# Splitting float32 weights inside the DMA transfers instead of on ScalarE and VectorE, in a two-layer transformer trunk

## The chip, the cores and the metric

One Trainium2 chip; the kernel runs on one of its cores. The metric is the device time in microseconds (us) of one execution. A core has TensorE (PE, matrix products; PEld is its weight loads), VectorE (DVE), ScalarE (ACT), GpSimd (POOL), SyncE (SP) and 16 DMA engines that all queues share. SP and ACT hand transfers to queue q1 and q10, POOL hands them to queue q0.

## What is computed

Two layers over 256 latent and 256 context tokens of width 1024. Each layer is a half step of a SwiGLU feed-forward net, a token mixing with four attention branches, and another half step. Each of the three starts with an RMS norm, scaled and shifted per feature. The last layer needs its second half step, and the queries of its mixing, for the latent half alone.

```python
D_MODEL, SEQ, CTX_LEN, DEPTH, D_FF = 1024, 256, 256, 2, 2816

def rmsnorm(x, g, eps=EPS):
    x32 = x.astype(jnp.float32)
    y = x32 * lax.rsqrt(jnp.mean(x32 * x32, axis=-1, keepdims=True) + eps)
    return (y * g.astype(jnp.float32)).astype(x.dtype)

def modulate(h, g, shift, scale):
    return rmsnorm(h, g) * (1 + scale) + shift

def swiglu(u, w_gu, w_down):
    g, up = jnp.split(u @ w_gu, 2, axis=-1)
    return (jax.nn.silu(g) * up) @ w_down

def gated_merge(u, ys, w_branch, w_gate, b_gate, w_out):
    terms = []
    for i, y in enumerate(ys):
        y = y.reshape(y.shape[:2] + (BRANCH_W,))
        terms.append(jax.nn.sigmoid(u @ w_gate[i] + b_gate[i]) * (y @ w_branch[i]))
    ...
    return merged @ w_out
```

All of it is float32. The kernel multiplies in the shorter format fp32r, and so writes each float32 operand as a high part (the value rounded to fp32r) and a low part (the rest). A product is the sum of three: high by high, high by low, low by high.

## The kernel before

Features lie on the 128 partitions and tokens along the free dimension: 512 columns where both halves run, 256 where the latent half runs alone. A **block** is 512 KB of weight, [128, 1024] (some are 384 KB and smaller). A full block makes 24 products, eight slices of 128 features by three (`mm3`, L132 to L138), and is used once. There are 414 blocks, all through `weights` (L119): SP loads a block into `wraw` (three buffers), ACT rounds it into `whi` (L127), DVE subtracts to get `wlo` (L128), and PE uses both. `whi` and `wlo` have five buffers each, so that weights are made up to five blocks ahead of PE.

The stages, by the time at which they run in the profiled execution: an opening (to about 47 us), the first half step of layer 0 (to about 390), its mixing (to 890), its second half step (to 1257), the first half step of layer 1 (to 1630), its mixing with 256 query columns (to about 1955), and its second half step with 256 columns. During the half steps of 512 columns but for the mixing, SP also loads 512 KB blocks `wa` of the modulation weights, which DVE multiplies and sums itself (L298).

Each engine works off its own list in order; a scheduler fixes the lists when the kernel is built, from the order in which the code asks for the work and from when buffers come free. A row `[waits PE_49]` in such a list says that the instruction waits for a count of PE's; DMASW and DMAHW are counts of transfers.

The factors 1/sqrt of the norms (`rsqrt_cols`, L140) are three Newton steps on tiles of 2 to 8 columns; by default POOL does them in twelve small instructions, in places VectorE in nine (`eng=nc.vector`). POOL also adds the branches (`merged`, L529), makes low parts of some heads (`ds`, L620), adds bias masks (`nab`, L708), and issues the SBUF-to-SBUF copies `kh`, `kl`, `mkh`, `mkl`.

## Time and profile before

| | |
|---|---|
| median of 2 runs | 2156.12 us (2155.53 to 2156.71) |
| span of the profiled execution, first to last instruction | 2153.2 us |
| PE busy | 2107.4 us, 98% |
| DVE busy | 1469.2 us, 68% |
| ACT busy | 911.8 us, 42% |
| POOL busy | 180.7 us, 8% |
| moved by DMA | 301.52 MB, 140 GB/s in the mean |

The profiled execution has no time of its own beside its span: the median of the runs is 2.9 us above the span, which is what lies around it. PE is close to always busy; the other engines and the DMA are busy in part, and by stage very differently, so their shares have to be read stage by stage.

### The profile page before, as it was taken

Reading aid. Unit: us, or ns where it says so; the run is one execution under the profiler, and the core shown is the slowest. Engines: PE = TensorE matmul, PEld = TensorE weight load, DVE = VectorE, ACT = ScalarE, POOL = GpSimd, SP = SyncE. Lnnn points to the kernel's source line nnn. Section 1 sums busy time; section 2 is a strip of 40 time slices with the busy share of each in tenths; the row PEclk is TensorE's granted clock in tenths of the full one; section 3 lists DMA queues with packets and bytes.
Section 4 is the critical chain, followed back from the end, with each engine's and each line's share of the span. In section 5 each row is a group of like instructions: output and inputs, shape, how many; then the busy total and the mean of one; then the engine's idle time right before and its main releaser. Section 6 shows DMA issues by size and latency. Waiting matters only on the chain.

```text
span 2153.2 us, 31572 instructions
## 1 busy us (share of the span) xinstructions
PE 2107.4 (98%) x12130; PEld 1805.8 (84%) x12130; DVE 1469.2 (68%) x2639; ACT 911.8 (42%) x1456; POOL 180.7 (8%) x322
## 2 busy tenths in 40 slices
PE   7999999999999999999999999999999999999998
PEld 5888888987777877988888898888889888999998
DVE  6776767678767665566665558767667887787655
ACT  3422222467655563432222233222225776765443
POOL 0000000110012112100000010000002433120000
PEclk9999999999999999999999999999999999999999
DMA  8555554241232223245444336555542335355553
GB/s 331 173 178 178 177 176 150 69 121 47 66 100 73 88 66 118 92 157 156 140 154 150 105 118 203 179 176 186 165 127 90 105 106 138 128 168 171 192 183 102
DMA packets 95207, 301.52 MB, mean 140 GB/s; under 512 B 18640, under 2 KB 20048, under 8 KB 94672
## 3 DMA queue, kind: packets, MB, share of 16 engines
q1 hardware_dynamic: 92080, 295.10, 43.0%
q0 software_dynamic: 2688, 4.20, 1.0%
q8 instruction: 96, 1.57, 0.3%
q14 instruction: 55, 0.45, 0.1%
q10 hardware_dynamic: 288, 0.20, 0.0%
HBM read 294.21 MB, written 1.05 MB: 137 GB/s over the span
## 4 chain that ended last, share of the span: by engine, by line
PE 89%; DVE 5%; ACT 2%; issue 1%; POOL 1%; DMA 1%; SPq 0%; DVEq 0%; POOLq 0%; ACTq 0%
PE pgu L134 13%; PE pgu L137 13%; PE pgu L138 13%; PE pd L137 6%; PE pd L138 6%; PE pd L134 6%; PE pgt L134 4%; PE pgt L137 4%; PE pgt L138 4%; PE av L789 2%; PE pj L134 2%; PE pj L137 2%; PE pj L138 2%; PE psS L735 2%; PE tps L775 1%
## 5 line engine op out<-in xcount | busy, mean ns | idle before, releaser
L127 ACT CAST whi<-wraw 128x1024 fp32r<-128x1024 f32 (+2 forms) x414 | 423.1, 1024 | 993.8 <-PE pgu L137 434.7
L128 DVE TENSOR_TENSOR wlo<-wraw,whi 128x1024 fp32r<-128x1024 f32 (+2 forms) x414 | 495.2, 1197 | 160.6 <-ACT whi L127 141.5
L134 PE MATMUL pgu<-uh,whi 128*128 128x512 f32 (+1 forms) x1440 | 511.9, 357 | 1.4 <-ACT sg L357 0.9
L137 PE MATMUL pgu<-ul,whi 128*128 128x512 f32 (+1 forms) x1440 | 512.7, 356 | 0.6 <-DVE ul L230 0.4
L138 PE MATMUL pgu<-uh,wlo 128*128 128x512 f32 (+1 forms) x1440 | 512.2, 356 | 0.0
L298 DVE SCALAR_TENSOR_TENSOR junk<-wa,sbc 128x1024 f32<-128x1024 f32 x256 | 312.3, 1220 | 3.1
L134 PEld LDWEIGHTS pgu<-uh,whi 128*128 128x128 f32 x1440 | 271.1, 189 | 43.4 <-issue 2.5
L137 PEld LDWEIGHTS pgu<-ul,whi 128*128 128x128 f32 x1440 | 272.1, 189 | 39.4 <-DVE ul L230 1.1
L138 PEld LDWEIGHTS pgu<-uh,wlo 128*128 128x128 f32 x1440 | 272.1, 189 | 39.1 <-DVE wlo L128 0.3
L137 PE MATMUL pd<-al,whi 128*128 128x512 f32 (+1 forms) x794 | 273.4, 344 | 0.2 <-DVE al L372 0.2
L134 PE MATMUL pd<-ah,whi 128*128 128x512 f32 (+1 forms) x794 | 273.5, 345 | 0.0
L138 PE MATMUL pd<-ah,wlo 128*128 128x512 f32 (+1 forms) x794 | 273.1, 344 | 0.0
L134 PE MATMUL pgt<-uh,whi 128*128 128x512 f32 (+1 forms) x512 | 176.5, 345 | 0.4 <-ACT cacc L548 0.4
L358 DVE TENSOR_TENSOR af<-sg,pgu 128x512 f32<-128x512 f32 (+1 forms) x86 | 53.6, 625 | 179.5 <-PE pgu L138 179.5
L137 PE MATMUL pgt<-ul,whi 128*128 128x512 f32 (+1 forms) x512 | 174.1, 340 | 0.0
L138 PE MATMUL pgt<-uh,wlo 128*128 128x512 f32 (+1 forms) x512 | 173.8, 339 | 0.0
L137 PEld LDWEIGHTS pd<-al,whi 128*128 128x128 f32 x794 | 149.3, 188 | 20.9 <-DVE al L372 0.9
L134 PEld LDWEIGHTS pd<-ah,whi 128*128 128x128 f32 x794 | 149.2, 188 | 20.0
L138 PEld LDWEIGHTS pd<-ah,wlo 128*128 128x128 f32 x794 | 149.1, 188 | 19.9
L336 DVE SCALAR_TENSOR_TENSOR h<-pd,mod,h 128x256 f32<-128x256 f32 x168 | 76.4, 480 | 105.7 <-PE pd L138 105.3
L148 POOL TENSOR_TENSOR rq<-ry 128x2 f32<-128x2 f32 (+2 forms) x48 | 12.1, 252 | 1252.5 <-DVE ry L146 1241.6
L134 PEld LDWEIGHTS pgt<-uh,whi 128*128 128x128 f32 x512 | 97.6, 191 | 13.2 <-issue 3.3
(240 smaller groups left out, 3125.2 us busy)
## 6 DMA issues: line engine op xcount, KB each, us to landing
wraw<-wgu SPq DMA_DIRECT2D x176, 512.0 KB, 3.3
wa<-wada SPq DMA_DIRECT2D x128, 512.0 KB, 4.2
wraw<-wd SPq DMA_DIRECT2D x64, 512.0 KB, 3.6
wraw<-wgate SPq DMA_DIRECT2D x64, 512.0 KB, 3.3
wraw<-win SPq DMA_DIRECT2D x28, 512.0 KB, 3.3
wraw<-wd SPq DMA_DIRECT2D x32, 384.0 KB, 3.1
w<-wada SPq DMA_DIRECT2D x16, 512.0 KB, 8.0
wraw<-wbr SPq DMA_DIRECT2D x16, 512.0 KB, 3.3
```

What stands on the lines that cost most here:

```text
L127: nc.scalar.copy(hi[:, :n], raw[:, :n])
L128: nc.vector.tensor_sub(lo[:, :n], raw[:, :n], hi[:, :n])
L134: ins = nc.tensor.matmul(ps, lh, rh, start=start, stop=False)
L137: nc.tensor.matmul(ps, lh, rl, start=False, stop=False)
L138: nc.tensor.matmul(ps, ll, rh, start=False, stop=stop)
L148: eng.tensor_mul(q[:, :n], y[:, :n], y[:, :n])
L298: ins = nc.vector.scalar_tensor_tensor(junk, w, 1.0, sbc[:, v], op0=ALU.mult, op1=ALU.mult, accum_out=m[:, t, v:v + 1])
L336: nc.vector.scalar_tensor_tensor(h[k][:, hv[0]:hv[1]], ps[:, off:off + S], gate[:, k, v:v + 1], h[k][:, hv[0]:hv[1]], op0=ALU.mult, op1=AL ...
L358: nc.vector.tensor_mul(af[:, :ntok], sg[:, :ntok], pu[:, :ntok])
L735: nc.tensor.matmul(ps[:, :nk], q_[:, q0:q0 + P], k_[:, self.k0:T], start=z == 0, stop=z == len(qs) - 1 and not bias_mm)
L775: nc.tensor.transpose(tps[:, b], self.p[:, b * P:(b + 1) * P], ident)
L789: nc.tensor.matmul(av[un.qt * 64:(un.qt + 1) * 64], V[br](u0.k0 // P + b, hd), un.pT[:, b], start=b == 0, stop=b == kt - 1)
```

## The change

`weights` no longer loads a block once. POOL issues a transfer from HBM into `whi`, which rounds on its way; ACT writes the negative of `whi` into `wlo`; POOL issues a second transfer of the same block, which adds the weight onto `wlo`. The buffer `wraw` is gone, and `whi` and `wlo` have six buffers instead of five. The Newton steps run on VectorE everywhere. The rest of the diff takes out comments. Line numbers after it are two or three lower: L125 and L127 are the transfers, L126 the negation, L132, L135 and L136 the products.

```diff
-    wp = es.enter_context(tc.tile_pool(name="wp", bufs=5))
+    wp = es.enter_context(tc.tile_pool(name="wp", bufs=6))
...
     def weights(src, shape):
         n = shape[1] * shape[2]
-        raw = wp.tile([P, 1024], F32, name="wraw", tag="wraw", bufs=3)
-        rv = raw[:, :n].rearrange("p (k c) -> p k c", k=shape[1])
-        nc.sync.dma_start(rv, src)
         hi = wp.tile([P, 1024], F32R, name="whi", tag="whi")
         lo = wp.tile([P, 1024], F32R, name="wlo", tag="wlo")
-        nc.scalar.copy(hi[:, :n], raw[:, :n])
-        nc.vector.tensor_sub(lo[:, :n], raw[:, :n], hi[:, :n])
-        return (hi[:, :n].rearrange("p (k c) -> p k c", k=shape[1]),
-                lo[:, :n].rearrange("p (k c) -> p k c", k=shape[1]))
+        hv, lv = [x[:, :n].rearrange("p (k c) -> p k c", k=shape[1]) for x in (hi, lo)]
+        nc.gpsimd.dma_start(hv, src)
+        nc.scalar.activation(lo[:, :n], hi[:, :n], AF.Copy, scale=-1.0)
+        nc.gpsimd.dma_start(lv, src, accum_op=ALU.add)
+        return hv, lv
...
-    def rms_cols(parts, ntok, dim, eps, heads=1, eng=nc.gpsimd, pin=False):
+    def rms_cols(parts, ntok, dim, eps, heads=1, eng=nc.vector, pin=False):
...
-        def cols(self, stats, hv, eng=nc.gpsimd):
+        def cols(self, stats, hv, eng=nc.vector):
...
-        def rest(self, stats, hv, between, eng=nc.gpsimd, rs=None):
+        def rest(self, stats, hv, between, eng=nc.vector, rs=None):
```

What this does to the lists is shown at three places. First the opening. SP's list before, where `wraw` are the blocks of weight and `w0` those of the first modulation:

```order
L1000 DMA w0_183<-wada0 128x1024 [waits DMAHW1_49]
L1000 DMA w0_189<-wada0 128x1024 [waits DMAHW2_49]
L124 DMA wraw_195<-wgu1 128x1024 [waits DMAHW3_49]
L124 DMA wraw_201<-wgu1 128x1024 [waits DMAHW4_49]
L1000 DMA w0_237<-wada0 128x1024 [waits DMAHW5_49]
L1000 DMA w0_243<-wada0 128x1024 [waits DMAHW6_49]
L1000 DMA w0_272<-wada0 128x1024 [waits DMAHW7_49]
L1000 DMA w0_278<-wada0 128x1024 [waits DMAHW0_49]
```

The two blocks of weight stand behind the first two `w0`, in one queue with all of them. POOL's list at the same place after the change (`ident` is a constant that POOL makes):

```order
L125 DMA whi_195<-wgu1 128x1024
masks.py:199 ISA
masks.py:199 AFFINE_SELECT ident_79<-ident_79 128x128 [waits Pool_49]
L127 DMA wlo_196<-wgu1 128x1024 [waits Activation_49]
L125 DMA whi_200<-wgu1 128x1024
L125 DMA whi_388<-wgu1 128x1024
L125 DMA whi_393<-wgu1 128x1024
L127 DMA wlo_201<-wgu1 128x1024 [waits Activation_49]
L127 DMA wlo_389<-wgu1 128x1024 [waits Activation_49]
L127 DMA wlo_394<-wgu1 128x1024 [waits Activation_49]
```

Eight transfers of four blocks now stand at the head of a queue of their own, beside SP's.

Next a stretch of the first half step of layer 0, SP's list before (`wgu1` are weights of the first half step, `wada` those of the modulation):

```order
L124 DMA wraw_1711<-wgu1 128x1024 [waits DMAHW2_49,DVE_49]
L124 DMA wraw_1718<-wgu1 128x1024 [waits DMAHW4_49,DVE_49]
L295 DMA wa_1547<-wada 128x1024 [waits DMAHW5_49,DVE_49]
L124 DMA wraw_1795<-wgu1 128x1024 [waits DMAHW6_49,DVE_49]
L124 DMA wraw_1802<-wgu1 128x1024 [waits DMAHW0_49,DVE_49]
L295 DMA wa_1623<-wada 128x1024 [waits DMAHW7_49,DVE_49]
L124 DMA wraw_1877<-wgu1 128x1024 [waits DMAHW1_49,DVE_49]
L295 DMA wa_1629<-wada 128x1024 [waits DMAHW2_49,DVE_49]
L124 DMA wraw_1884<-wgu1 128x1024 [waits DMAHW3_49,DVE_49]
```

A block is one row here, held back until a buffer `wraw` comes free. POOL's list in that half step after the change:

```order
L125 DMA whi_1451<-wgu1 128x1024 [waits DMASW6_49,PE_49]
L127 DMA wlo_1452<-wgu1 128x1024 [waits DMASW7_49,Activation_49]
L125 DMA whi_1525<-wgu1 128x1024 [waits DMASW0_49,PE_49]
L125 DMA whi_1531<-wgu1 128x1024 [waits DMASW1_49,PE_49]
L127 DMA wlo_1526<-wgu1 128x1024 [waits DMASW2_49,Activation_49]
L127 DMA wlo_1532<-wgu1 128x1024 [waits DMASW3_49,Activation_49]
L125 DMA whi_1605<-wgu1 128x1024 [waits DMASW4_49,PE_49]
L127 DMA wlo_1606<-wgu1 128x1024 [waits DMASW5_49,PE_49,Activation_49]
L125 DMA whi_1611<-wgu1 128x1024 [waits DMASW6_49,PE_49]
```

A block is two rows now, and the second (`wlo`) waits for ACT's negation, with the next `whi` queued behind it: first one block by itself (`whi`, `wlo`), then two together (`whi`, `whi`, `wlo`, `wlo`), and so on in threes.

Last the second half step of layer 1, with 256 columns. SP's list before:

```order
L124 DMA wraw_19228<-wgu2 128x1024 [waits DMAHW6_49,DVE_49]
L124 DMA wraw_19235<-wgu2 128x1024 [waits DMAHW7_49,DVE_49]
L124 DMA wraw_19298<-wgu2 128x1024 [waits DMAHW0_49,DVE_49]
L124 DMA wraw_19305<-wgu2 128x1024 [waits DMAHW1_49,DVE_49]
L124 DMA wraw_19368<-wgu2 128x1024 [waits DMAHW2_49,DVE_49]
L124 DMA wraw_19375<-wgu2 128x1024 [waits DMAHW3_49,DVE_49]
L124 DMA wraw_19438<-wgu2 128x1024 [waits DMAHW4_49,DVE_49]
```

Here too a block is one row and waits for nothing but a free buffer. POOL's list there after the change:

```order
L125 DMA whi_19328<-wgu2 128x1024 [waits DMASW6_49,PE_49]
L125 DMA whi_19390<-wgu2 128x1024 [waits DMASW7_49,PE_49]
L125 DMA whi_19396<-wgu2 128x1024 [waits DMASW0_49,PE_49]
L127 DMA wlo_19329<-wgu2 128x1024 [waits DMASW1_49,Activation_49]
L127 DMA wlo_19391<-wgu2 128x1024 [waits DMASW2_49,Activation_49]
L127 DMA wlo_19397<-wgu2 128x1024 [waits DMASW3_49,Activation_49]
L125 DMA whi_19458<-wgu2 128x1024 [waits DMASW4_49,PE_49]
L125 DMA whi_19464<-wgu2 128x1024 [waits DMASW5_49,PE_49]
L125 DMA whi_19526<-wgu2 128x1024 [waits DMASW6_49,PE_49]
```

Here three `whi` go out together and then three `wlo`, so that the next three `whi` stand behind the last of three negations.

## Rows read from the trace of the kernel before

**Rows 1.** The page, busy us and instructions of each engine.

```profile
PE 2107.4 (98%) x12130; PEld 1805.8 (84%) x12130; DVE 1469.2 (68%) x2639; ACT 911.8 (42%) x1456; POOL 180.7 (8%) x322
```

**Rows 2.** The page, the chain that ended last, by engine.

```profile
PE 89%; DVE 5%; ACT 2%; issue 1%; POOL 1%; DMA 1%; SPq 0%; DVEq 0%; POOLq 0%; ACTq 0%
```

**Rows 3.** The page, costliest groups: the split of the weights.

```profile
L127 ACT CAST whi<-wraw 128x1024 fp32r<-128x1024 f32 (+2 forms) x414 | 423.1, 1024 | 993.8 <-PE pgu L137 434.7
L128 DVE TENSOR_TENSOR wlo<-wraw,whi 128x1024 fp32r<-128x1024 f32 (+2 forms) x414 | 495.2, 1197 | 160.6 <-ACT whi L127 141.5
```

**Rows 4.** Busy us of the engines, clock, DMA share and rate in seven stretches.

```profile
core 0: us, PE busy (x) PEld busy (x) DVE busy (x) ACT busy (x) POOL busy (x), PEclk, DMA share, GB/s
0.00:53.80 53.80, 39.18 (x259) 27.13 (x260) 32.71 (x95) 20.95 (x33) 0.70 (x6) 1.00 0.88 331
60.00:380.00 320.00, 320.00 (x1414) 263.11 (x1413) 229.20 (x351) 88.22 (x113) 0.00 (x0) 1.00 0.55 173
400.00:880.00 480.00, 472.04 (x2628) 383.38 (x2627) 326.21 (x683) 269.77 (x491) 71.12 (x112) 1.00 0.28 85
900.00:1250.00 350.00, 349.56 (x1646) 291.87 (x1645) 209.65 (x320) 97.85 (x131) 2.41 (x12) 1.00 0.44 140
1290.00:1620.00 330.00, 329.56 (x1480) 271.95 (x1479) 233.54 (x354) 90.93 (x115) 0.00 (x0) 1.00 0.54 171
1660.00:1950.00 290.00, 282.94 (x2137) 257.84 (x2137) 233.18 (x474) 198.74 (x349) 83.08 (x120) 0.99 0.44 133
2000.00:2100.00 100.00, 100.00 (x838) 99.79 (x837) 57.42 (x69) 42.26 (x54) 0.00 (x0) 1.00 0.58 185
```

**Rows 5.** PE's own waits: us in total, times, longest.

```profile
PE ps L177 <- POOL ry L155: 5.2, 4, 1.9
PE tps L775 <- DVE pexp L764: 7.8, 11, 1.9
```

**Rows 6.** Line L127 in six stretches: count, duration ns, first and last start.

```profile
L127 ACT CAST whi<-wraw x5: 1032/1045/1052, 14.6 to 42.2; 128x1024 fp32r<-128x1024 f32 x5
L127 ACT CAST whi<-wraw x60: 835/1053/1057, 61.2 to 376.8; 128x1024 fp32r<-128x1024 f32 x52, 128x768 fp32r<-128x768 f32 x8
L127 ACT CAST whi<-wraw x67: 622/1049/1111, 400.7 to 869.2; 128x1024 fp32r<-128x1024 f32 x58, 128x768 fp32r<-128x768 f32 x5, 128x864 fp32r<-128x864 f32 x2, 128x576 fp32r<-128x576 f32 x1
L127 ACT CAST whi<-wraw x64: 835/1053/1061, 899.3 to 1244.3; 128x1024 fp32r<-128x1024 f32 x56, 128x768 fp32r<-128x768 f32 x8
L127 ACT CAST whi<-wraw x63: 835/1053/1061, 1292.9 to 1614.4; 128x1024 fp32r<-128x1024 f32 x55, 128x768 fp32r<-128x768 f32 x8
L127 ACT CAST whi<-wraw x67: 622/1047/1064, 1664.1 to 1948.5; 128x1024 fp32r<-128x1024 f32 x61, 128x768 fp32r<-128x768 f32 x5, 128x512 fp32r<-128x512 f32 x1
```

**Rows 7.** DMA issues (count, size, us to landing): all; 60 to 380; 900 to 1250.

```profile
wraw<-wgu SPq DMA_DIRECT2D x176, 512.0 KB, 3.3
wa<-wada SPq DMA_DIRECT2D x46, 512.0 KB, 4.2
wa<-wada SPq DMA_DIRECT2D x30, 512.0 KB, 3.4
```

**Rows 8.** DMA queues in 1660 to 1950: packets, MB, share of 16 engines.

```profile
q1 hardware_dynamic: 14206, 36.04, 40.2%
q0 software_dynamic: 1344, 2.10, 3.5%
```

**Rows 9.** POOL's issue of a DMA (busy, mean ns, then idle before it).

```profile
L665 POOL DMA_DIRECT2D kh<-kh x12 | 6.7, 561 | 78.7 <-ACT kh L662 78.7
```

**Rows 10.** Timeline 388 to 398: the same POOL instruction beside DVE and alone.

```profile
390.72 1.23 DVE L128 TENSOR_TENSOR wlo<-wraw,whi 128x1024 fp32r<-128x1024 f32 x1 [0.21 <-ACT whi L127]
390.87 1.13 POOL L153 TENSOR_TENSOR rq<-rq,rv 128x2 f32<-128x2 f32 x1
392.96 0.20 POOL L153 TENSOR_TENSOR rq<-rq,rv 128x2 f32<-128x2 f32 x1
```

## Prediction

> **What bounds the kernel now.** I read first the page's busy times: PE works 2107.4 of 2153.2 us, DVE 1469.2, POOL 180.7 [rows 1]. Then the chain that ended last: 89% of it is PE, 5% DVE, 1% POOL [rows 2]. So PE's pace sets the time, and all that a faster VectorE could give back lies in 46 us of PE's idle time, 2.1%. The table by stretches says where it lies [rows 4]: 14.6 us in the first 53.8, 8 in the mixing of layer 0, 7 in that of layer 1, next to none in the half steps. The same table says what carries the change: the DMA engines are 0.88 busy in the opening, about 0.55 in the first half steps, 0.28 and 0.44 in the mixings, 0.58 in the last half step. The last reading is of the counts of blocks in each stretch [rows 6], from which PE's pace per block follows.
>
> A full block is 24 products. In 60 to 380 a product takes 320 us / 1414 = 0.226 us, so a block 5.43; in the last half step 100 / 838 = 0.119, so a block 2.86 [rows 4]. In the mixings the stretch divided by its blocks is 480 / 67 = 7.16 us (layer 0) and 290 / 67 = 4.33 us (layer 1) [rows 4, 6]. A weight path that needs longer than this for each block stops PE.
>
> **What the change takes away.** DVE loses 414 subtractions, 495.2 us [rows 3]. PE hardly waited for them, so they are worth little in time. The negation takes the place of ACT's rounding; I cost it at that row's 1.05 us. The rstd chains leave POOL, where PE waited 5.2 us for them in all; its waits for DVE's `pexp` come to 7.8 us [rows 5]. I take 10 us of gain for both, between 0 and 21 (POOL's 1% of the chain, [rows 2]).
>
> **What it adds: the price of a transfer.** The DMA engines' full rate is 331 GB/s / 0.88 = 376 GB/s in the busiest stretch [rows 4], so a block (524,288 bytes) takes 1.39 us of all 16. From issue to landing a load takes 3.3 us [rows 7], hence 1.91 us beyond the moving. An issue on POOL takes 0.56 us [rows 9]. The first transfer I cost like a load, 1.39. The second adds onto what lies in `wlo`, and no row shows such a transfer. It costs at least what it costs to load the weight, 1.39 us. The upper bound is the load plus a whole copy from SBUF to SBUF: queue q0 moved 2.10 MB of such copies in 3.5% of 290 us, 10.2 us of all engines, so 2.53 us a block [rows 8], 3.92 together. The old `wlo` has to be read besides the weight, but written only once, so I take two loads, 2.78 us.
>
> The Trainium skill has the rule for this: in "Collectives: The Full Stack", section "The bandwidth ceiling: the fold count and why AG ≠ RS ≠ AR", an add in the DMA path is slower because it reads two sources on one ring, and not because of the adding; it gives 62.28 GB/s for a copy against 32.35 with an add, a factor of 1.93. By that factor the second transfer would take 2.68 us and my sum would come out some 25 us lower. No run shown here has such a transfer.
>
> **The round trip on POOL's list.** DMA capacity alone is not the limit in the early half steps, but POOL's list is in order, and a `wlo` waits there for ACT with the next `whi` behind it. I follow one group of three blocks as the list has it (whi, wlo, whi, whi, wlo, wlo), the DMA taken as one server of 376 GB/s. First `whi`: moved 0.56 to 1.95, landed 3.86, negated 4.91, its `wlo` issued 5.47 and moved until 8.25. The second and third `whi` stand behind that and are moved until 9.64 and 11.03; the second lands 11.55, is negated 12.60, its `wlo` goes out 13.16 and moves until 15.94, the third until 18.72, where the next group begins. A group thus takes 18.16 us, 6.05 a block, against PE's 5.43: 0.62 too long. The modulation loads lie on top. There are 46 for 60 blocks [rows 6, 7], so 1.07 us a block, of which half should fall into the DMA's gaps (1.95 to 5.47 and 11.03 to 13.16 above, 5.65 us a group): 0.53 more. In 60 to 380 that is 1.15 x 60 = 69 us; in 900 to 1250, with 30 such loads, 0.95 x 64 = 61; in 1290 to 1620, with again 46, 1.13 x 63 = 71. Together 201. Each of these stages begins with weights five blocks ahead, 27 us, of which a block's way through both transfers uses 10; the other 17 are eaten up before PE waits. 201 - 51 = **150 us**.
>
> **Last half step.** The group is three `whi`, then three `wlo`. The first `wlo` goes out at 5.47, the three are moved until 13.81, where the next group begins: 13.25 us, 4.42 a block against 2.86. This is now plainly the DMA's own limit (4.17 of moving a block). The code asks for 68 blocks here; four are wanted early and some three more lie ready, and eight of the rest are 384 KB, which leaves 59 full ones: 1.56 x 59 = 92, less 4 of lead, **88 us**.
>
> **Mixing of layer 1.** A block needs 4.17 us of DMA where PE's pace is 4.33, so it just fits. But POOL's own adds, 83 us in this stretch [rows 4], now stand in one list with the transfers. If they were all in the way it would cost 83 us, if none 0; **30 us**, since they leave gaps of POOL's 290. In layer 0's mixing 6.05 is under 7.16: nothing.
>
> **Opening.** The DMA has 12% of 53.8 us free there, 6.5. Five blocks were rounded in it [rows 6]; with six begun, six second transfers and one more first one are 18.1 us. PE waits for the `w0` behind them: **12 us**, between 0 (hidden in the 14.6 us of idle PE) and 18.
>
> **Sum.** 150 + 88 + 30 + 12 - 10 = 270 us on 2153.2, so a span of 2423; with 2.9 us around it **2426 us**, 12.5% more. What a measurement can tell here from no change is about 2%, 2113 to 2199 us.
>
> With the second transfer at 1.39 us the group of the half steps takes 4.66 a block (5.19 with half the modulation loads), which fits; the last half step 3.03 against 2.86, 5 us after the lead; the mixing 15, the opening 3: 2153 + 13 + 3 = **2169**. At 3.92 the group takes 7.19 a block, 366 us in the three half steps; the last one 5.56, 156; the mixing 0.98 x 67 + 30 = 96; the opening 18: **2782**.
>
> **Rivals.** (1) *The adding transfer moves at the price of a plain load.* Then every round trip fits PE's pace and the time is 2169, not slower than before. It decides at the second transfer's moving time: with it under about 1.6 us PE stays the bound. For it: nothing here shows that reading SBUF and HBM for one transfer cannot overlap. Against it: a 512 KB load already runs the engines at their full rate.
> (2) *Rounding on the way costs as much as adding.* The first transfer would take 2.78 us and the second 4.17, 6.95 a block and 2877 us for 414 blocks, above PE's pace in all stages but one; with the modulation loads about **3000 us**. Nothing in the trace speaks for or against, since none of its transfers changes the format.
> (3) *POOL's issues are held up by VectorE.* The same POOL instruction takes 1.13 us beside a subtraction of DVE's and 0.20 alone [rows 10]. Were each issue 0.9 us longer, 1.48, the group would take 5.36 us a block even with plain loads; with half the modulation loads 0.46 too long, 35 us after the lead, and the time about **2210**. Against it: `kh` issues take 0.56 us in the mean with DVE busy around them [rows 9]. In the Trainium skill, "SBUF — State Buffer", section "Who interferes with whom", transfers issued from GpSimd starve for descriptors while VectorE, in a two-port mode (a float32 copy within SBUF, for one), holds the ports that both share; by that rule the cost falls where VectorE copies, and no run shown here has a POOL issue that starved.
> (4) *The idle of PE goes.* All of it would be 46 us, 2110: faster by just over 2%. The weights would have to come sooner than now with twice the transfers.
>
> **How the numbers follow.** My forecast (second transfer at 2 to 3.9 us, 2250 to 2800) 0.48; rival 1 0.24; rival 2 0.18; rival 3 0.07; rival 4 0.03. The time is that of the likeliest, 2426. The range goes down to 2165, past most of rival 1, and up to 2850, just above the upper bound of the add; what is left out is rival 2, the lower part of rival 1 and rival 4. Slower by over 2%: 0.48 + 0.18 + 0.07 and a quarter of rival 1, 0.79; within 2%: 0.18; faster: 0.03.
>
> **What the profile after should show.** DMA share near 0.9 or more in the half steps, and 1.0 with PE idle in 2000 onward; PE waiting for DMA `wlo`, which it never did for weights; queue q0 with some 420 MB in place of 4.20; L127 landing some 1.5 us later than L125; L126 at about 1.05 us; DVE near 980 us. PE should stay whole in layer 0's mixing. If q0's `wlo` land as fast as `whi`, rival 1 holds; if `whi` themselves take 5 us or more from an idle DMA, rival 2; if POOL's issues exceed 1 us, rival 3. I am wrong altogether if PE's idle lies at POOL's own instructions rather than at transfers: then the list is at fault and not the DMA.

## The result, and where the time went

The kernel after takes **2662.16 us** (2660.36 to 2663.97, 2 runs) against 2156.12 (2155.53 to 2156.71): a ratio of **1.2344**, 95% interval 1.2308 to 1.238. It is slower, as forecast and inside the range; the forecast of 2426 us had about half of the 506 us that were lost. The profiled execution has a span of 2658.6 us.

The page of the kernel after, in the order of [rows 1]: busy time and share of PE, the granted clock and the DMA share in 40 slices, then the queues.

```profile
PE 2259.5 (85%) x12130; PEld 1901.9 (72%) x12130; DVE 1040.8 (39%) x2369; ACT 909.9 (34%) x1458; POOL 693.1 (26%) x958
...
PEclk8989898999999999989999898989889989898887
DMA  9887877574566667677787778888767789999997
...
q0 software_dynamic: 121920, 424.73, 68.1%
```

PE has 399.1 us of idle time (2658.6 - 2259.5) in place of 45.8, so 353 of the 505 us of span are new idle time. The other 152 are a surprise: PE's *busy* time has grown from 2107.4 to 2259.5 us with the same 12130 products. The clock line says why: it now falls to 8 again and again, where the page before has 9 in every slice.

```profile
PEclk9999999999999999999999999999999999999999
```

The mean granted clock is 0.997 before and 0.923 after. PE's busy time multiplied by it is 2101 us before and 2086 after, so the lower clock accounts for the growth.

The table by stages (the columns as in [rows 4]) has its borders at the products of the norms' sums (`acc`, L162, L164 before). Before, these stand at 389.6, 886.5, 1259.2, 1627.2 and 1950.6 us.

```profile
core 0: us, PE busy (x) PEld busy (x) DVE busy (x) ACT busy (x) POOL busy (x), PEclk, DMA share, GB/s
0.00:494.30 494.30, 402.02 (x1778) 317.46 (x1778) 197.85 (x396) 117.91 (x159) 99.62 (x145) 0.91 0.81 219
494.30:1044.60 550.30, 506.76 (x2754) 410.36 (x2754) 272.99 (x686) 275.48 (x502) 149.51 (x194) 0.96 0.62 141
1044.60:1503.50 458.90, 393.51 (x1833) 323.80 (x1833) 149.49 (x295) 104.99 (x144) 97.37 (x137) 0.93 0.75 190
1503.50:1957.10 453.60, 387.58 (x1772) 317.63 (x1772) 188.73 (x361) 106.63 (x145) 96.26 (x135) 0.92 0.79 206
1957.10:2350.10 393.00, 338.97 (x2390) 309.32 (x2391) 183.40 (x506) 213.93 (x378) 156.75 (x216) 0.92 0.83 193
2350.10:2658.60 308.50, 230.68 (x1606) 223.31 (x1604) 48.31 (x130) 90.93 (x130) 93.61 (x132) 0.86 0.92 223
```

Length less PE busy is the idle time of a stage; the same view of the trace before gives the other side. In us:

| stage | longer by | of it PE idle | of it PE busy | forecast |
|---|---|---|---|---|
| opening and first half step | 104.7 | 77.7 | 27.0 | 12 + 52 |
| mixing, layer 0 | 53.4 | 34.2 | 19.2 | 0 |
| second half step | 86.2 | 64.9 | 21.3 | 44 |
| first half step, layer 1 | 85.6 | 63.2 | 22.4 | 54 |
| mixing, layer 1 | 69.6 | 46.0 | 23.6 | 30 |
| last half step | 105.9 | 67.2 | 38.7 | 88 |

(The 52, 44 and 54 are the prediction's 69, 61 and 71 less 17 each, its 150.)

The waits of PE (us, times, longest), which in [rows 5] had no weight in them:

```profile
PE pd L132 <- ACT ah L369: 123.1, 19, 15.8
PE pgu L136 <- DMA wlo<-wgu: 60.0, 33, 3.9
PE pgu L132 <- ACT sg L355: 32.7, 12, 5.4
PE av L787 <- ACT PT L775: 29.3, 12, 6.2
PE pd L136 <- DMA wlo<-wd: 29.0, 13, 4.2
```

PE does wait for `wlo`, but it waits longer for ACT, of which the prediction said nothing. By stages the two are apart. In the three half steps of 512 columns (the first from 60 us on) PE waits 165 us for ACT and 28 for transfers, in the last half step 5 and 64. The two longest waits of the second half step (1044.6 to 1503.5), then of the last (2350.1 to the end):

```profile
PE pd L132 <- ACT ah L369: 41.0, 6, 15.8
PE pgu L132 <- ACT sg L355: 10.5, 4, 5.2
```
```profile
PE pgu L136 <- DMA wlo<-wgu: 38.1, 17, 3.9
PE pd L136 <- DMA wlo<-wd: 22.8, 8, 4.2
```

POOL's list in the first half step (start, length, idle time before it and its releaser), and ACT's list beside it:

```profile
207.36 0.85 POOL L127 DMA_DIRECT2D wlo<-wgu  x1 [9.42 <-ACT wlo L126]
207.90 1.43 POOL L125 DMA_DIRECT2D whi<-wgu  x2
215.28 0.88 POOL L127 DMA_DIRECT2D wlo<-wgu  x1 [5.95 <-ACT wlo L126]
216.67 0.87 POOL L127 DMA_DIRECT2D wlo<-wgu  x1 [0.51 <-ACT wlo L126]
217.22 0.88 POOL L125 DMA_DIRECT2D whi<-wgu  x1
225.66 0.85 POOL L127 DMA_DIRECT2D wlo<-wgu  x1 [7.57 <-ACT wlo L126]
```
```profile
213.92 1.06 ACT L126 ACTIVATE wlo<-whi 128x1024 fp32r<-128x1024 f32 x1 [6.85 <-DMA whi<-wgu]
215.31 1.06 ACT L126 ACTIVATE wlo<-whi 128x1024 fp32r<-128x1024 f32 x1 [0.33 <-DMA whi<-wgu]
216.27 0.58 ACT L355 ACTIVATE sg<-pgu 128x512 f32<-128x512 f32 x1
224.31 1.06 ACT L126 ACTIVATE wlo<-whi 128x1024 fp32r<-128x1024 f32 x1 [7.46 <-DMA whi<-wgu]
225.28 0.60 ACT L369 CAST ah<-af 128x512 fp32r<-128x512 f32 x1
```

The group of three blocks is there as forecast: from the `wlo` at 207.36 to the one at 225.66 are 18.30 us. This is the shortest of the 45 such groups in the three half steps of 512 columns; their mean is 20.30. The prediction has 18.16 without the modulation loads and 19.1 to 19.7 with half of them. And ACT shows the second wait: `ah`, whose input DVE wrote at 216.88 to 217.57, stands behind a negation that waits 7.46 us for `whi`, and runs at 225.28. Whether that costs PE time of its own, or is the same lateness seen from another side, the page doesn't say.

### The profile page after: what moved, and what is told of

Same layout as the page of the kernel before. It is cut to its first block, busy times and chain, and to the rows that moved or that the text cites. A ratio compares the mean times of both kernels' runs of the same rounds, so it can differ in the third digit from the quotient of the medians.

```text
span 2658.6 us, 31838 instructions
## 1 busy us (share of the span) xinstructions
PE 2259.5 (85%) x12130; PEld 1901.9 (72%) x12130; DVE 1040.8 (39%) x2369; ACT 909.9 (34%) x1458; POOL 693.1 (26%) x958
## 3 DMA queue, kind: packets, MB, share of 16 engines
q0 software_dynamic: 121920, 424.73, 68.1%
HBM read 504.45 MB, written 1.05 MB: 190 GB/s over the span
## 5 line engine op out<-in xcount | busy, mean ns | idle before, releaser
L126 ACT ACTIVATE wlo<-whi 128x1024 fp32r<-128x1024 f32 (+2 forms) x414 | 426.1, 1032 | 1390.5 <-DMA whi<-wgu 630.7
L136 PE MATMUL pgu<-uh,wlo 128*128 128x512 f32 (+1 forms) x1440 | 524.3, 367 | 55.3 <-DMA wlo<-wgu 55.2
L132 PE MATMUL pgu<-uh,whi 128*128 128x512 f32 (+1 forms) x1440 | 527.0, 367 | 44.1 <-ACT sg L355 32.7
L135 PE MATMUL pgu<-ul,whi 128*128 128x512 f32 (+1 forms) x1440 | 524.2, 365 | 0.0
L132 PE MATMUL pd<-ah,whi 128*128 128x512 f32 (+1 forms) x794 | 296.9, 374 | 135.4 <-ACT ah L369 123.1
L136 PEld LDWEIGHTS pgu<-uh,wlo 128*128 128x128 f32 x1440 | 281.4, 197 | 104.4 <-DMA wlo<-wgu 39.4
L127 POOL DMA_DIRECT2D wlo<-wgu x176 | 153.0, 871 | 762.3 <-ACT wlo L126 664.2
L132 PEld LDWEIGHTS pgu<-uh,whi 128*128 128x128 f32 x1440 | 282.1, 196 | 92.1 <-ACT sg L355 37.5
L136 PE MATMUL pd<-ah,wlo 128*128 128x512 f32 (+1 forms) x794 | 291.9, 371 | 29.0 <-DMA wlo<-wd 29.0
L135 PEld LDWEIGHTS pgu<-ul,whi 128*128 128x128 f32 x1440 | 283.0, 197 | 40.4 <-DVE mod L1012 0.8
L135 PE MATMUL pd<-al,whi 128*128 128x512 f32 (+1 forms) x794 | 295.2, 372 | 1.0 <-DVE al L370 0.9
L132 PEld LDWEIGHTS pd<-ah,whi 128*128 128x128 f32 x794 | 165.1, 208 | 168.2 <-ACT ah L369 133.7
L136 PEld LDWEIGHTS pd<-ah,wlo 128*128 128x128 f32 x794 | 164.7, 209 | 53.1 <-issue 22.8
L127 POOL DMA_DIRECT2D wlo<-wd x96 | 83.6, 881 | 449.8 <-ACT wlo L126 394.5
L370 DVE TENSOR_TENSOR al<-af,ah 128x512 fp32r<-128x512 f32 (+1 forms) x88 | 55.0, 625 | 367.8 <-ACT ah L369 367.7
L136 PE MATMUL pgt<-uh,wlo 128*128 128x512 f32 (+1 forms) x512 | 177.1, 347 | 12.2 <-DMA wlo<-wgate 12.2
L135 PEld LDWEIGHTS pd<-al,whi 128*128 128x128 f32 x794 | 164.7, 207 | 29.3 <-DVE al L370 8.6
L132 PE MATMUL pgt<-uh,whi 128*128 128x512 f32 (+1 forms) x512 | 178.6, 349 | 0.0
L135 PE MATMUL pgt<-ul,whi 128*128 128x512 f32 (+1 forms) x512 | 177.0, 346 | 0.0
```

Of the source, the lines that this page charges most:

```text
L126: nc.scalar.activation(lo[:, :n], hi[:, :n], AF.Copy, scale=-1.0)
L127: nc.gpsimd.dma_start(lv, src, accum_op=ALU.add)
L132: ins = nc.tensor.matmul(ps, lh, rh, start=start, stop=False)
L135: nc.tensor.matmul(ps, lh, rl, start=False, stop=False)
L136: nc.tensor.matmul(ps, ll, rh, start=False, stop=stop)
L370: nc.vector.tensor_sub(al[:, :ntok], af[:, :ntok], ah[:, :ntok])
```

## Experiments

All are variants of the kernel after (the "changed kernel"), unless said otherwise. Those with one time are one profiled run each, beside 2154 to 2159 us for the kernel before on the same chips. PE idle is the span less PE's busy time.

The scheduler builds the lists of every variant anew. In the traces e2_plain has every engine's list in the order of the changed kernel, and e13_both every list of e8_noland. The others differ: e8_noland's POOL list goes block by block (`whi`, `wlo`) where the changed kernel has groups of three.

| run | time, us | PE idle | PE busy |
|---|---|---|---|
| before | 2156.1 | 45.8 | 2107.4 |
| changed | 2662.2 | 399.1 | 2259.5 |
| e2_plain: second transfer without add | 2261.5 | 114.8 | 2144.9 |
| e8_noland: no list waits for a landing | 2246.5 | 107.6 | 2137.1 |
| e13_both: both of these | 2153.2 | 44.8 | 2106.6 |
| e11_poolwait: e8, POOL's wait given back | 2789.7 | 486.0 | 2301.9 |
| e12_actwait: e8, ACT's wait given back | 2313.9 | 154.0 | 2158.1 |
| e4_noadd: no second transfer | 2169.4 | 56.3 | 2111.4 |
| e3_negdve: negation on VectorE | 2738.6 | 456.7 | 2280.1 |
| e9_half: every second block as before | 2326.7 | 158.2 | 2166.6 |
| e7_hybrid: rounding transfer, subtraction on VectorE | 2225.4 | 94.0 | 2127.7 |
| e5_rstdpool: rstd back on POOL | 2702.0 | 423.7 | 2276.5 |
| e1_rstd: before, rstd on VectorE | 2159.2 | 45.2 | 2114.7 |

### The price of a transfer

**e10_price** has nothing of the network: only transfers, 24 blocks of each kind, one kind after the other. Here the rounding and the adding ones (`r` is fp32r, `f` float32):

```diff
+    for i in range(24):
+        nc.gpsimd.dma_start(v(r[i % 6]), blocks[i])
...
+    for i in range(24):
+        nc.gpsimd.dma_start(v(r[i % 6]), blocks[i], accum_op=ALU.add)
```

> Transfers alone, nothing of the network is computed: 24 blocks of 512 KB of each kind, onto six buffers in turn. Plain by SP, plain by POOL, rounding by POOL, adding in float32, adding with rounding, and plain by SP beside adding. From the packets of the changed kernel I expect 1.35 to 1.45 us a block for the first three, 2.5 to 2.8 for the adds with and without rounding, and the pair at their sum, 3.9 to 4.2. If the add is dear because of the format, the adding in float32 falls to 1.4. An issue on POOL: 0.53 us without, 0.85 with an add.

Five stretches: plain by SP, rounding by POOL, adding in float32, adding with rounding, and plain by SP beside adding. The last two numbers are DMA share and GB/s.

```profile
6.00:26.00 20.00, 0.00 (x0) 0.00 (x0) 1.00 1.02 410
68.00:90.00 22.00, 0.00 (x0) 9.32 (x19) 1.00 1.17 409
105.00:140.00 35.00, 0.00 (x0) 12.19 (x15) 1.00 1.07 211
165.00:200.00 35.00, 0.00 (x0) 12.23 (x15) 1.00 1.07 211
240.00:280.00 40.00, 0.00 (x0) 9.43 (x11) 1.00 1.06 276
```

A block of 524,288 bytes takes 1.28 us plain (524,288 / 410 GB/s), 1.28 rounding and 2.48 adding, with or without a change of format. A plain and an adding block side by side take 2 x 524,288 / 276 GB/s = 3.80, their sum. So rounding is free and adding costs 1.94 times a load. (Shares a little above 1 I read as a full DMA.) All three prices lie just below the ranges that I expected, and the adding in float32 did not fall to 1.4, so the format is not what makes the add dear. An issue on POOL takes 0.53 us for a rounding transfer and 0.86 for an adding one.

**e2_plain** takes the add out of the changed kernel.

```diff
-        nc.gpsimd.dma_start(lv, src, accum_op=ALU.add)
+        nc.gpsimd.dma_start(lv, src)
```

> The changed kernel, its second transfer without the add: the low part becomes the rounded weight, the subtraction is left out. Every engine's list is the same as in the changed kernel, so only the moving time of the second transfer differs. Theory A (the add's moving time, 2.62 us of all engines for a block in place of 1.4, sets the loss): the group round trip falls under PE's pace, packets of q0 take one time (about 174 ns), the time is 2170 to 2250, PE's granted clock near 0.99. Theory B (waiting lists set the loss: a second transfer waits on POOL for the negation, and ACT's copies stand behind a negation that waits for a landing; the moving time matters little): over 2400, with the second transfer still behind the negation 313 times.

2261.5 us, 11 above the upper end of Theory A's range: with every list unchanged, 401 of the 506 us go. The second transfers still stand behind the negation (L127 waits 573.2 us on ACT's for `wgu` alone), so what is left, 105 us, is still the waits (e13_both below has the same transfers without them, and none of the loss): 49 of them in the last half step (251.3 us in place of 202.6).

**e4_noadd** leaves the second transfer out.

```diff
-        nc.gpsimd.dma_start(lv, src, accum_op=ALU.add)
```

> The changed kernel without its second transfer: the low part stays the negative of the high part, the subtraction is left out. Theory A: the DMA has 1.4 us for a block and POOL's list holds nothing that waits for ACT, so the time is 2130 to 2165, with PE as whole as in the kernel before. Theory B in its ACT half (copies of the feed-forward behind a negation that waits for a landing): 2200 or more, PE waiting for ACT's sg and ah as in the changed kernel.

2169.4 us, PE idle 56.3: 4 above Theory A's range, and 31 under Theory B's. ACT's negations still wait for `whi` there (866.9 us, 337 times) and PE waits for ACT in next to nothing (`uh` 3.6 us, `PT` 1.9). So ACT's waiting list alone does next to no harm while one plain transfer is all that a block needs; Theory B's ACT half falls for this case. Some 7 us of the 13 lie before the end of the first half step (396.3 us in place of 389.6), where PE waits 19.1 us for the first modulation's `w` against 12.4 before.

### The wait

**e8_noland** keeps the add and all traffic, and takes the wait for `whi` out of both lists.

```diff
-        nc.scalar.activation(lo[:, :n], hi[:, :n], AF.Copy, scale=-1.0)
+        nc.scalar.activation(lo[:, :n], ones[:, 0:1].to_broadcast([P, n]), AF.Copy, scale=-1.0)
```

> The changed kernel, but ScalarE writes minus one from a constant into the low part instead of the negated high part, so this write no longer waits for the high part's landing. All transfers, the add and ScalarE's work stay; the low part's value is left out. The run with a plain second transfer put some 400 of the 505 us on the add. Theory B (the add costs mostly through the round trip: whi lands, negation, wlo waits at the head of POOL's list): the half steps of 512 columns come back to within 15 us each, since their DMA share of 0.78 to 0.80 then fits beside PE, the last half step stays about 100 us too long at a DMA share near 0.96, and the time is 2260 to 2340. Theory A (moving alone): the DMA is just as late without that wait, 2550 or more.

2246.5 us, just faster than Theory B's range: 416 of the 506 us go, with every adding transfer in place. The stretch 60 to 300 of this kernel, which had PE 217.29 busy at a DMA share of 0.80 in the changed one:

```profile
60.00:300.00 240.00, 240.00 (x1066) 196.65 (x1065) 123.30 (x226) 68.11 (x86) 63.42 (x90) 1.00 0.99 269
```

PE is whole and the DMA full. What is left is the last half step (253.7 us in place of 202.6, about half of the 100 expected), the mixing of layer 1 (341.0, 323.4 before) and the opening.

**e13_both** makes both changes, and closes the square.

> Both repairs together: the second transfer without the add and the low part written from a constant, so that no list waits for a landing (the low part's value is left out). It closes the square of price and wait. If the loss is the round trip made long by the add, each repair alone took nearly all of it and both together leave only the doubled traffic: 2160 to 2190, the last half step within 15 us of before. If two separate losses had been added, 2247 and 2261 would have left 1850 here, which PE's own work forbids.

2153.2 us, below the range expected, and no slower than before (2159.35 us in the run beside it): with twice the weight traffic (424.73 MB on q0), the DMA at 0.75 to 0.84 in the half steps of 512 columns (the first with the opening) and 0.97 in the last, and PE whole. Against the trace before it is 7.8 us longer in the opening and first half step and 1.0 to 4.2 us shorter in each other stage. So neither traffic, nor POOL's issues, nor ACT's 901 us cost anything here in sum.

| | waits for the landing | does not wait |
|---|---|---|
| adding | 2662 | 2247 |
| plain | 2261 | 2153 |

The two losses don't add up: the wait costs 108 us with quick transfers and 416 with slow ones. The loss is a round trip, and the add is what makes it long. The rows of the square compare equal work, but its columns differ in more than the wait: without it the lists come out in another order too. That this order is not the cure is shown by the next run, which also goes block by block there.

**Whose wait?** **e11_poolwait** gives e8_noland a wait for `whi` on POOL, and none on ACT.

```diff
         nc.scalar.activation(lo[:, :n], ones[:, 0:1].to_broadcast([P, n]), AF.Copy, scale=-1.0)
+        nc.gpsimd.tensor_copy(lo[:, 0:1], hi[:, 0:1])
         nc.gpsimd.dma_start(lv, src, accum_op=ALU.add)
```

> The kernel of e8_noland (low part written from a constant, its value left out) with one thing given back: POOL copies one column of the high part into the low part ahead of the second transfer, so POOL's list waits for whi's landing, and ScalarE's does not. POOL then works one block at a time. By hand: wlo out at 0.86 us, moved to 3.35, the next whi moved to 4.63, landed 6.5, so some 6.8 us a block. If POOL's wait is what stops PE, the half steps of 512 columns are as late as in the changed kernel or later and the time is 2600 to 2900. If ScalarE's list is needed for the loss, the time stays at 2250 to 2400.

2789.7 us, in the range for POOL's wait, and 543 above e8_noland, with ACT's list the same in all but 18 of 1455 places. (The 414 one-column copies keep POOL itself busy for 118.5 us.) In 60 to 300 it makes 794 products, 33.1 blocks, 7.25 us a block (6.8 by hand), at a DMA share of 0.72. Its list works one block at a time where the changed kernel's has groups of three, so it shows that POOL's wait alone is enough, not how much of the 506 it is. PE's waits are now where the cause is:

```profile
PE pgu L137 <- DMA wlo<-wgu: 201.5, 122, 6.9
PE pd L137 <- DMA wlo<-wd: 157.4, 81, 5.0
```

The last half step of this run shows the cure by accident. There the list has the next `whi` ahead of each `wlo`:

```profile
2609.85 0.18 POOL L127 CAST wlo<-whi 128x1 fp32r<-128x1 f32 x1 [1.82 <-DMA whi<-wgu]
2610.30 0.55 POOL L125 DMA_DIRECT2D whi<-wgu  x1 [0.26 <-issue]
2610.83 0.91 POOL L128 DMA_DIRECT2D wlo<-wgu  x1
2613.63 0.18 POOL L127 CAST wlo<-whi 128x1 fp32r<-128x1 f32 x1 [1.89 <-DMA whi<-wgu]
```

A block every 3.78 us (2609.85 to 2613.63), the DMA's own 1.28 + 2.48, and this stage takes 260.4 us (2527.5 to 2787.9) where the changed kernel needs 308.5. So a `wlo` that waits costs little in this stage if one `whi` is always under way ahead of it: 7 us over the 253.7 of e8_noland, where no list waits.

**e12_actwait** gives e8_noland the wait on ACT instead.

```diff
         nc.scalar.activation(lo[:, :n], ones[:, 0:1].to_broadcast([P, n]), AF.Copy, scale=-1.0)
+        nc.scalar.copy(see[:, 0:1], hi[:, 0:1])
         nc.gpsimd.dma_start(lv, src, accum_op=ALU.add)
```

> The kernel of e8_noland with the other half given back: ScalarE, after writing the low part from a constant, copies one column of the high part into a spare tile, so that ScalarE's list waits for every whi's landing with sg, ah and PT behind it, and the second transfer on POOL does not wait for it. If ScalarE's list is a cause of its own, PE waits for ah and sg as in the changed kernel and the time is over 2400. If it only shows lateness that POOL's list makes, the time stays within 40 us of e8_noland's 2247.

2313.9 us, 67 above e8_noland: between the two forecasts, so neither holds as it stands. ACT's wait costs something by itself, far less than POOL's; some of the 67 may be the copies of `see`, with which ACT is busy for 53 us more. The rows where the changed kernel has 123.1 us of `ah`, 44.2 of `sg` and 29.3 of `PT` now read

```profile
PE av L790 <- ACT PT L778: 21.9, 6, 8.4
PE pd L135 <- ACT ah L372: 15.2, 5, 6.9
```

and 30 of the 67 us lie in the mixing of layer 1 (371.2 us against 341.0), where softmax goes through ACT.

**e3_negdve** moves the negation off ACT.

```diff
-        nc.scalar.activation(lo[:, :n], hi[:, :n], AF.Copy, scale=-1.0)
+        nc.vector.tensor_scalar(lo[:, :n], hi[:, :n], -1.0, None, op0=ALU.mult)
```

> The changed kernel with the negation on VectorE in place of ScalarE. ACT's list then holds nothing that waits for a weight. If PE's waits for ACT (ah 123 us, sg 44 us, PT 29 us) are a cause of their own, most of them go and the time falls by 100 us or more, to about 2500 or below. If they only show that the DMA is late (Theory A), the waits move to DVE's af and al or to wlo, and the time stays within 60 us of 2662. If VectorE's negations hold up POOL's transfers, the issues grow beyond 0.87 us and the time rises.

2738.6 us, slower by 76, outside the 60 that Theory A allowed, and no fall. The negation is quicker (692 ns against 1032 in the mean over all shapes), yet it waits for `whi` at the head of the list that makes `af`, and PE waits for that:

```profile
PE pd L132 <- ACT ah L369: 148.1, 19, 15.4
PE pgu L132 <- DVE af L356: 71.2, 29, 5.5
```

ACT is named first still, with a list in which no weight stands: its `ah` waits 928.8 us for DVE's `af`. The releaser of a wait is the last messenger. POOL's issues for `wgu` grew a little (`wlo` 913 ns in the mean, 871 in the changed kernel). In the trace, 74 of the 414 issues of `wlo` overlap a negation and take 1.03 us in the mean, the other 340 take 0.89. That is some 10 us of issues, so VectorE may hold POOL up, but far too little for the 76.

**e9_half** does every second block the old way.

```diff
-        nc.gpsimd.dma_start(hv, src)
-        nc.scalar.activation(lo[:, :n], hi[:, :n], AF.Copy, scale=-1.0)
-        nc.gpsimd.dma_start(lv, src, accum_op=ALU.add)
+        if nwt[0] % 2:
+            nc.gpsimd.dma_start(hv, src)
+            nc.scalar.activation(lo[:, :n], hi[:, :n], AF.Copy, scale=-1.0)
+            nc.gpsimd.dma_start(lv, src, accum_op=ALU.add)
+        else:
+            raw = wp.tile([P, 1024], F32, name="wraw", tag="wraw", bufs=2)
+            nc.sync.dma_start(raw[:, :n].rearrange("p (k c) -> p k c", k=shape[1]), src)
+            nc.scalar.copy(hi[:, :n], raw[:, :n])
+            nc.vector.tensor_sub(lo[:, :n], raw[:, :n], hi[:, :n])
```

> Every second block by the changed way, the others as before (loaded by SP, rounded by ScalarE, subtracted by VectorE); rstd on VectorE; five buffers for the parts and two for the raw weight. A block then takes 2.75 us of all DMA engines in the mean and POOL has two blocks' time for a round trip. If the rule is that the path must fit PE's pace (5.43, 4.33 and 2.86 us a block), all stages fit and the time is 2160 to 2200. If a waiting list stops PE whatever the mean load is, over 2250.

2326.7 us: my rule "the path must fit PE's mean pace" (2160 to 2200) fails, and the other forecast holds, a waiting list that stops PE (over 2250). The edit also takes one of the six buffers away. POOL still waits 908.9 us for ACT (151 times), and old and new blocks share ACT's list, so an old block's rounding stands behind a new block's landing. 63 of the 171 us lie in the last half step and 51 in the mixing of layer 1.

**e7_hybrid** has no add: POOL's rounding transfer for the high part, SP's load and VectorE's subtraction for the low one.

```diff
-        nc.scalar.activation(lo[:, :n], hi[:, :n], AF.Copy, scale=-1.0)
-        nc.gpsimd.dma_start(lv, src, accum_op=ALU.add)
+        raw = wp.tile([P, 1024], F32, name="wraw", tag="wraw", bufs=3)
+        nc.sync.dma_start(raw[:, :n].rearrange("p (k c) -> p k c", k=shape[1]), src)
+        nc.vector.tensor_sub(lo[:, :n], raw[:, :n], hi[:, :n])
```

> High part by the rounding transfer, the weight itself loaded a second time by SP into a buffer of its own, low part by VectorE's subtraction as before: no add in a transfer and nothing on ScalarE. DMA 2.9 us a block, and no list in which a transfer waits for an engine's result. By the price theory every stage fits but the last half step, which is level (2.9 against 2.86): 2150 to 2180. If rounding transfers beside loads are slower than alone, or landing order matters, over 2200.

2225.36 us, a ratio of 1.033 (95% interval 1.0307 to 1.0353): slower than I gave it. This edit too has five buffers for the parts in place of six, which was not tried apart. 35 of some 69 us lie in the mixing of layer 1 (358.6 us, 323.4 before), 13 in that of layer 0. VectorE's subtractions wait for landings there in the list that also holds softmax. That these waits are the cause was not tried by itself.

### The other part: rstd

**e1_rstd** is the kernel before with the default engine of the rstd chains VectorE, as in the diff; **e5_rstdpool** is the changed kernel with it on POOL.

> The kernel before with only its rstd chains moved from POOL to VectorE; the weights stay as before. The prediction gave this and the freed DVE together 10 us, at most 21. PE waited 5.2 us for those chains, so I expect 2150 to 2156, at best 0.3 per cent faster; a rival: the nine instructions queue on VectorE behind subtractions, 2156 to 2165.

> The changed kernel with its rstd chains back on POOL, as before the change. If the move to VectorE was needed, since on POOL a chain stands behind transfers that wait, each of the five norms and the small ones of the mixing end later and the time rises by 20 to 80 us over 2662. If the chains find gaps, it stays within 15 us.

e1_rstd: 2159.15 us, ratio 1.0013 (1.0004 to 1.0022), in the rival's range. A tenth of a per cent slower, not 10 us faster: PE's idle time is the same (45.2 us), its waits for `ry` 6.4 us in place of 9.1 by either engine. e5_rstdpool: 2702.0 us in one run, 40 slower than the changed kernel. A chain in POOL's list now stands behind transfers that wait, so the move to VectorE is worth some 40 us in the new kernel and nothing in the old.

## Why the prediction was right, and where its sizes were off

**Right: direction and price.** The adding transfer costs two loads: 2.78 us by the prediction, 2.48 measured, since the full rate is 410 GB/s and not the 376 that I had from a stretch at a share of 0.88. Rivals 1 and 2 fall with e10_price. The rule of the Trainium skill that the prediction weighed ("Collectives: The Full Stack", section "The bandwidth ceiling: the fold count and why AG ≠ RS ≠ AR"), two sources read on one ring, a factor of 1.93, agrees with the trace: 410 / 211 GB/s is 1.94. That the second read is the reason, no run shows. Rival 3 falls: the issues of L127 for `wgu` and `wd` take 0.87 and 0.88 us in the mean, and that is the add's own price, the same with VectorE idle (0.86 in e10_price). Rival 4 falls with PE's 399 us.

**Useless: the signs by landing.** `wlo` was to land some 1.5 us later than `whi`; the page has 5.4 us from issue to landing for `wlo` and 7.6 for `whi` (of `wgu`). Read by the prediction's own signs, that would speak for rival 1, and with an idle DMA for rival 2 as well. These times also hold what stands ahead in the queue, and only e10_price separates the two.

**Right in size, in part by luck: the round trip's pace, and the lead.** How far each start of a PE product lies behind the same product of the trace before, from the start of its stage, in us:

| stage | after 200 products | after 500 | after 1600 | at the end |
|---|---|---|---|---|
| opening and first half step | 13.6 | 13.6 | 68.7 | 104.7 |
| second half step | 6.9 | 7.0 | 56.9 | 86.2 |
| first half step, layer 1 | 3.6 | 3.7 | 57.5 | 85.6 |

From 500 to 1600 are 46 blocks, so PE falls behind by 1.20, 1.09 and 1.17 us a block; the prediction had 1.15, 0.95 and 1.13. From 200 to 500 it loses nothing: that is the lead. The three terms come to 159 us against 150, and the opening to 13.6 against 12. But with the prices as measured (1.28 and 2.48 us) the same sum by hand gives 17.0 us a group in place of 18.16, and the trace has 20.30 in the mean: transfers priced too dear made up for a part of the delay that was left out. e8_noland and e11_poolwait show that the wait makes this loss: taken out of both lists, with the order that comes with that, it gives back 416 us, and in POOL's list alone it stops PE. "I am wrong altogether if PE's idle lies at POOL's own instructions" was badly put: the list and the DMA are not alternatives, since each alone costs about 100 us.

**Wrong: what PE waits for in these half steps.** The prediction let PE wait for `wlo`. It waits for `ah` and `sg`, 165 us against 28: they stand in ACT's list behind a negation that waits for its `whi`. ACT's list is a term that the prediction left out; it costed the negation at 1.05 us (1.03 measured) and asked what it takes, not what stands behind it while it waits. The pace came out right all the same. As I read it, that is because ACT's list and POOL's wait for each other and go at one pace, that of the round trip. How much is due to each list in the changed kernel is not shown.

**Missing: the end of each half step.** After the 1600th product another 36.0, 29.3 and 28.1 us are lost, 93 in all. POOL's list there no longer goes in threes, as the prediction had it throughout, but block by block:

```profile
446.29 0.86 POOL L127 DMA_DIRECT2D wlo<-wd  x1 [7.34 <-ACT wlo L126]
453.49 0.85 POOL L127 DMA_DIRECT2D wlo<-wd  x1 [5.79 <-ACT wlo L126]
```

A block of 384 KB takes 7.2 us here, and PE waits 13.1 us for an `ah` at 461.57. e8_noland loses nothing at these places, e2_plain 7 to 12 us at each.

**Wrong: "every round trip fits PE's pace" with quick transfers.** For a second transfer at the price of a load the prediction had 2169 us. e2_plain is that kernel, and it takes 2261.5. What the sum lacks even there is the ends of the half steps, the mixing of layer 1 (+14.7 us) and most of the last half step (+48.7).

**Wrong: "DMA share near 0.9 or more in the half steps".** It is 0.75 to 0.81 in those of 512 columns. A list that waits leaves the DMA idle; e8_noland, without the wait, fills it (0.99 in 60 to 300).

**Wrong: "in layer 0's mixing nothing", and 30 in layer 1's.** They take 53 and 70 us longer. The mean pace of 7.16 us fits a round trip of 6.05, but in the mixings ACT's list holds softmax, `PT` and the negations together: in layer 0's PE waits 29 us for ACT and 3 for transfers. Of the 53 us e12_actwait gets 15, e11_poolwait 30, e8_noland 1.5: both lists take part. The reason given for the 30, POOL's own adds in the list, is not borne out: they stand there in e13_both too, which loses nothing in this stage.

**Off: the last half step.** 106 us longer against 88, at 4.54 us a block against 4.42, so the size is nearly right. But it is not "plainly the DMA's own limit": that is 3.76 us a block and not 4.17, the share is 0.92, and e8_noland and e11_poolwait, which reach the limit, lose 51 and 58.

**Missing: the clock.** The forecast had no term for it. In the changed kernel PE stops from 218.3 on:

```profile
216.00:218.00 2.00, 2.00 (x11) 1.57 (x9) 0.69 (x1) 0.85 (x2) 1.49 (x3) 1.00 0.55 86
218.00:220.00 2.00, 0.31 (x2) 0.00 (x0) 0.00 (x0) 0.00 (x0) 0.10 (x1) 1.00 1.09 203
220.00:222.00 2.00, 1.54 (x6) 1.27 (x7) 0.00 (x0) 0.00 (x0) 0.00 (x0) 0.89 1.04 203
222.00:224.00 2.00, 2.00 (x7) 1.52 (x6) 0.00 (x0) 0.00 (x0) 0.00 (x0) 0.50 0.88 295
224.00:226.00 2.00, 2.00 (x8) 1.64 (x7) 0.09 (x1) 1.57 (x2) 0.34 (x1) 0.75 0.00 0
226.00:228.00 2.00, 2.00 (x10) 1.65 (x10) 1.97 (x4) 0.00 (x0) 1.64 (x3) 1.00 0.45 41
```

After the gap the granted clock (the third number from the end) is 0.50 of 2.4 GHz, that is 1.2 GHz, for a stretch in which PE is busy throughout, and then full again. In the nine kernels with more than 40 us of new idle time and the same products, PE's busy time grows by 0.42 to 0.54 us for each us of it: 0.43 in the changed kernel (152.1 / 353.3), 0.44 in e11_poolwait (194.5 / 440.2), 0.54 in e2_plain (37.5 / 69.0), 0.48 in e8_noland (29.7 / 61.8). That is a relation over runs; the clock itself was not set by any of them. Nor does it follow that 152 us would be saved at full clock: where a list sets the pace, a quicker PE would only wait longer, and the round trip's pace above holds without a term for the clock.

**Not seen: 10 us of gain.** The rstd chains are worth -2.5 us by themselves. The freed VectorE may be part of the 1.0 to 4.2 us by which e13_both is shorter in five stages, but the opening takes most of that back, and this is one run. DVE's busy time of 1040.8 us (forecast 980) also holds the chains that came to it.

By terms, forecast and measured: opening 12 and 13.6; the half steps from their 500th to their 1600th product 150 and 159; what the two later ones lose before that 0 and 11; the ends of all three 0 and 93; the mixings 30 and 123; the last half step 88 and 106. Together 280 and 505. So the forecast is low by the ends and the mixings, 186 of the 235 us that it lacks; the round trip came out at its size.

## What to carry to other kernels

When a step moves from "load, then compute" to "transfer, compute, transfer", price the round trip on the in-order list that issues the transfers, and look for a list in which the next first transfer always stands ahead of the waiting second one: the same traffic took 2662 us with the wait and 2247 without it. Follow that list to the end of each stage, where its pattern may change. Ask of every instruction that waits for a landing what stands behind it, on whichever engine it is put; moving it from ScalarE to VectorE only moved the victims. Where PE stands still in many gaps, expect its busy time to grow as well (by 0.42 to 0.54 us per us of idle time in these nine kernels), but don't add that to a time that comes from the pace of a list.

## What the runs showed of the hardware that was not expected

- A transfer that rounds float32 on its way moves at the plain rate: 409 against 410 GB/s. One that adds moves at 211, whether it rounds or not; a plain and an adding stream together make 276 GB/s, so neither hides the other.
- Adding costs POOL time too: an issue of `wlo` for `wgu` takes 0.53 us in e2_plain and 0.87 with the add.
- Two transfers per block in place of one, all issued by POOL, cost nothing in sum where no list waited: 2153.2 us, with a DMA share of 0.97 in the last half step and up to 369 GB/s in a slice of it.
- VectorE negates 128x1024 in 709 ns where ScalarE takes 1059, and the kernel is slower with it.
